# A square block of values with tokens on partitions, kept in DRAM by rows, in a hybrid decoder block on one Trainium2 core

## The chip, the cores and the metric

The kernel runs as one program on one core of a Trainium2 chip. The time is in device microseconds, from the start to the end of an execution on that core. Its engines are TensorE (PE in the profile; its weight loads are PEld), VectorE (DVE), ScalarE (ACT), GpSimd (POOL) and SyncE (SP), which here does little but issue DMAs.

## The reference, cut to what matters

One layer with 1024 tokens, model width 1024, everything in fp32:

```python
h = rms_norm(x, mix_norm_g)                       # (1024 tokens, 1024)
z_a, q, k, v, gate_logits = split(h @ w_in)       # 1536 | 768 | 768 | 768 | 2048 columns
# A: z_a = gelu(z_a); u, v_z = its halves; v_z = rms_norm(v_z) over 768 channels,
#    mixed over chunks of 128 tokens by w_spatial, times u
# B: attention in 3 groups of 4 heads (dilation 1, 4, 16), partial rotary on q and k;
#    the outputs of the groups are mixed by their softmax denominators
merged = sigmoid(g_A) * (y_A @ P_A) + sigmoid(g_B) * (y_B @ P_B)
x = x + merged @ w_out
x = x + (gelu(causal_conv3(h2 @ w_gate)) * (h2 @ w_val)) @ w_down     # h2 = rms_norm(x)
out = rms_norm(x, final_norm_g)
```

The change lies in `h @ w_in` and in what takes over its results.

## The kernel before, in words

**Products.** A fp32 product is made of three passes of fp32r matmuls: each operand is split into a high part (a copy on ACT) and a low part (the difference, on DVE), and high x high, low x high and high x low are added up in PSUM. On top of that the large products use a Strassen scheme with 7 products P1 to P7 in place of 8, on quarters of the operands. For the input projection, x stands transposed (channels on partitions), and its sums of quarters (A11, S2, A12, ...) are made once. The columns of w_in come in pairs of 128: for each pair, in_product (L534) runs P1 to P7, each of 12 matmuls of 128x512 (4 slices of the contraction by 3 passes), with weights as the stationary operand and x as the moving one, so that a result has channels on partitions and 512 tokens in the free dimension. The operand of a product is made ahead: weight sums on DVE (L278 to L288), its high part on ACT (L313), its low part on DVE (L314), in four slots. in_evict (L560) adds the products up on DVE and ACT, and in_final (L645) passes results on.

**The order of pairs.** Values of the gating branch (zv) come first. Two of their three pairs are "lead" pairs: lead_pass (L609, matmuls L618) computes them without Strassen with tokens on partitions while the sums of x are made. The third (FIRST) goes through in_product, and because the spatial mixing needs tokens on partitions, turn_v turns it with 16 PE transposes of 128x128 (L681, copied out by ACT at L682). Then come per attention group g = 1, 2, 0 the pairs qa, qc (queries and keys) and v, whose 256 columns attention() turns likewise with 16 transposes per group (L967, ACT L969); then eight gate pairs (ga) with the three pairs zu after the fourth.

**Work beside the products.** tick() is called after every 6 matmuls (half a product); after(lag, fn) puts a step lag ticks later. So the order of PE's instructions is written out: norm_v (L697: square on ACT, the factor rs_v on POOL, scaling on DVE at L709), spatial (L713: 12 small matmuls pm in two PSUM banks per block of 128 tokens, taken out by DVE at L738), and the steps of Attend (L814: load q and k from DRAM, turn them into parts, scores sc at L863 and L867, softmax, pp = transposed probabilities, pT = their copy out of PSUM at L920 on ACT or L922 on DVE, pu = the product with v at L935). mix_groups (L1033) mixes the outputs of the groups with strided operations on DVE (L1072, L1074); while it runs, wd_step makes the sums of w_down's quarters for its first three slices of the contraction (L1144). The other sums, two per step ff, are made beside the up products of the last stage by wd_beside; each sum is stored to DRAM as wT.

**Queues.** All of PE is in written order. DVE and ACT are in written order from the start to the 18th product (ORDERED); from there a scheduler places their instructions. SP issues nearly all DMAs, in order. PSUM has three banks for accumulators (acc), two for turning and small products (tr, which pm uses too) and, in the first part, three more (ps_d).

Of the kernel before, what the change touches and what calls it, by code (L numbers as in the profile page):

```python
# [11 lines left out]
F32 = mybir.dt.float32  # L12
# [8 lines left out]
P = 128  # L21
# [16 lines left out]
FIRST = 2  # L38
SW = 2 * NH
# [20 lines left out]
def input_pairs():  # L60
# [12 lines left out]
    for p in range(3):  # L73
        pairs.append(("zv", p))
        cols += run(OFF_V + 256 * p, 256)
    for g in GROUPS:
        pairs += [("qa", g), ("qc", g), ("v", g)]
        lead, then = range(0, 8), range(8, 16)
        for dims in (lead, then, range(16, 32)):
            cols += by_dim(OFF_Q, g, dims) + by_dim(OFF_K, g, dims)  # L80
        cols += by_dim(OFF_Q, g, range(32, 64)) + by_dim(OFF_K, g, range(32, 64))
        cols += run(OFF_VV + 256 * g, 256)
    for dt in (0, 1, 2, 3, "zu", 4, 5, 6, 7):
        if dt == "zu":
            for p in range(3):
                pairs.append(("zu", p))
                cols += run(OFF_U + 256 * p, 256)
        else:
            pairs.append(("ga", dt))
            cols += run(OFF_G + P * dt, P) + run(OFF_G + D + P * dt, P)  # L90
    return pairs, cols
# [3 lines left out]
def block_kernel(  # L95
# [15 lines left out]
    w_lead: bass.AP,  # L111
    out: bass.AP,
# [145 lines left out]
    C.append(cxp.tile([P, 2, 1024], F32, name="C2"))  # L258
    OPS_IN = 4
# [66 lines left out]
    ORDERED = 18  # L326
    in_order = [(FIRST, name) for name in ("P1", "P2", "P6", "P7", "P5", "P4")]
    in_order += [(FIRST + 1, "P1"), (FIRST, "P3")]
    in_order += [(FIRST + 1, name) for name in ("P2", "P6", "P7", "P5", "P4", "P3")]
    for n in range(FIRST + 2, NP_IN):  # L330
        in_order += [(n, name) for name in ("P1", "P6", "P2", "P7", "P5", "P4", "P3")]
# [11 lines left out]

    def sums_ahead(i):
        if 7 < i <= ORDERED and in_order[in_ready["op"]] not in summed:
            in_sums(*in_order[in_ready["op"]])
# [159 lines left out]
    def c_tile(n):  # L506
        if n < 5:
            return C[2] if n == FIRST else zv["C"][n - 3]
        return C[(n + 1) % 2]

    def c_half(n, i, h):
        kind, g = PAIRS[n]
        t = c_tile(n)[:, i]
        if kind in ("qa", "qc", "v") and g == 1:
            return t.rearrange("p (r b j) -> p b r j", r=4, b=2)[:, h]
        if kind in ("qa", "qc", "v") and g == 2:
# [3 lines left out]
    def in_turn(n, ap):  # L520

        kind, g = PAIRS[n]
        if kind in ("qa", "qc", "v") and g:
# [3 lines left out]
    FUNC = {"zv": AF.Gelu, "zu": AF.Gelu}  # L527
# [3 lines left out]

    held = []

    def in_product(n, name):  # L534
# [3 lines left out]
        elif name == "P1" or n >= 3:  # L538
            acc = acc_tile(f"in_{n}_{name}")
        else:  # L540
            acc = ps_d.tile([P, HALF], F32, name=f"in_{n}_{name}", tag="dn")
# [11 lines left out]
        if (n, name) == (FIRST, "P4"):  # L553
            held.append(lambda: in_evict(n, name, acc))
        else:
            in_evict(n, name, acc)
            while held:
                held.pop()()
# [86 lines left out]
    def in_final(n, i, h):  # L645
# [3 lines left out]
        if kind == "zv":  # L649
            if (i, h) in ((0, 1), (1, 0)):  # L650
                for bb in range(2):
                    after(5 + bb if h else 4 + bb, lambda b=4 * h + 2 * bb: turn_v(ct, b))
            if (i, h) == (1, 0):
                for b in range(NB):
                    after(7 + 2 * b, lambda b=b: norm_v(b))
                    after(12 + 2 * b, lambda b=b: spatial(b))
        elif kind == "qa":
# [8 lines left out]
        elif kind == "v":  # L666
            if (i, h) == (1, 0):
                attention(p, ct)
# [7 lines left out]
    def turn_v(ct, b):  # L676

        pt = tr_tile(f"vt_{b}")
        for k in range(4):
            o = (b + k // 2) * P  # L680
# [1926 lines left out]
```

## Time and profile before

| | |
|---|---|
| time, median of 3 runs | 1341.72 us (1341.5 to 1342.11) |
| profiled execution | 1342.39 us |
| its span, first to last instruction | 1339.9 us |
| granted TensorE clock | 0.999 of full speed |
| DMA | 241.68 MB, mean 180 GB/s |
| DVE busy, share in the span's 40 slices | 5 to 9 tenths |

In a row of the profile, "L545 PE MATMUL in_P<-R,G 128*128 128x512 f32 x1008 | 237.5, 391 | 0.0" means line 545 of the kernel, engine, operation, output and inputs by tile name without buffer numbers, their shape, the count; then busy us in total, mean ns of one; then the idle time of the engine just before them, with the instruction that ended it. Rows of the waits give what waited, for whom, the total, the number and the longest. The chain is the work that ended last, followed backwards; its rows are start, us, what. Rows of a timeline are start, us, engine, line, operation. Rows of a table of stretches give the stretch, its length and the busy us of PE, PEld, DVE, ACT and POOL (with instruction counts), the granted clock, DMA's share and GB/s.

### The profile page before, as it was taken

What the parts mean: (1) busy time and instruction counts of PE and PEld (TensorE: products, weight loads), DVE (VectorE), ACT (ScalarE), POOL (GpSimd) and SP (SyncE); (2) the same over time, 40 slices, a digit from 0 to 9 for tenths busy, and PEclk for the clock granted to TensorE, in tenths of its full rate; (3) what the DMA queues carried; (4) which work ended last, traced back from release to release, by engine and by line L of the source; (5) the groups of instructions that cost most, each with busy time, mean ns of one, the idle gap of its engine ahead of it and who ended that gap; (6) DMA issues with size and microseconds to landing.
All of it is one profiled execution on the core that took longest, in us unless ns stands there. A gap on an engine that the chain in (4) does not pass through costs nothing.

```text
span 1339.9 us, 18988 instructions
## 1 busy us (share of the span) xinstructions
PE 1327.4 (99%) x6391; PEld 1098.3 (82%) x6391; DVE 1043.4 (78%) x1807; ACT 640.0 (48%) x1242; POOL 281.4 (21%) x271
## 2 busy tenths in 40 slices
PE   9999999999999999999999999999999999999997
PEld 8887887888887888888888788888888888888886
DVE  7988796877779957768889789777777778586674
ACT  7762566666633325345365333433343335454453
POOL 1120000000000000210010336656565653000002
PEclk9999999999999999999999999999999999999999
DMA  9437554555349733975550334454445538996663
GB/s 354 108 103 186 166 152 145 145 155 156 126 134 241 255 127 129 315 232 202 190 166 17 126 101 157 159 165 165 163 151 175 177 116 298 379 336 215 197 204 125
DMA packets 155714, 241.68 MB, mean 180 GB/s; under 512 B 22785, under 2 KB 66274, under 8 KB 155618
## 3 DMA queue, kind: packets, MB, share of 16 engines
q1 hardware_dynamic: 153378, 236.50, 54.8%
q0 software_dynamic: 1088, 2.10, 0.9%
q10 hardware_dynamic: 1152, 1.89, 0.4%
q8 instruction: 50, 0.82, 0.3%
q14 instruction: 46, 0.38, 0.1%
HBM read 172.03 MB, written 64.73 MB: 177 GB/s over the span
## 4 chain that ended last, share of the span: by engine, by line
PE 93%; DVE 3%; ACT 1%; DMA 1%; issue 1%; SPq 1%; POOL 0%; POOLq 0%; DVEq 0%; ACTq 0%
PE in_P L545 26%; PE uP L2020 20%; PE dn L2302 15%; PE up L2020 9%; PE wo_P L1851 5%; PE pa L1481 5%; PE pl L618 3%; PE pu L2000 2%; PE pb L1481 2%; PE pu L935 1%; PE pp L914 1%; PE pm L733 1%; PE sc L863 1%; DMA wr<-in_w_in_dram 1%; PE ht L1755 1%
## 5 line engine op out<-in xcount | busy, mean ns | idle before, releaser
L545 PE MATMUL in_P<-R,G 128*128 128x512 f32 x1008 | 237.5, 391 | 0.0
L545 PEld LDWEIGHTS in_P<-R,G 128*128 128x128 f32 x1008 | 187.3, 188 | 39.3 <-issue 0.5
L2302 PE MATMUL dn<-R 128*128 128x512 f32 x924 | 209.6, 389 | 0.0
L2302 PEld LDWEIGHTS dn<-R 128*128 128x128 f32 x924 | 173.4, 188 | 36.0
L313 ACT ACTIVATE G<-wr 128x512 fp32r<-128x512 f32 x126 | 78.3, 627 | 98.7 <-PE in_P L545 53.5
L170 ACT ACTIVATE R<-up 128x512 fp32r<-128x512 f32 x109 | 65.8, 623 | 123.6 <-DVE up L280 105.5
L2020 PE MATMUL uP<-G,R 128*128 128x512 f32 x504 | 121.3, 389 | 0.8 <-DVE Y L2041 0.8
L545 PE MATMUL in_P<-G,G 128*128 128x512 f32 x504 | 120.8, 392 | 0.6 <-DVE C L580 0.4
L2020 PE MATMUL uP<-R 128*128 128x512 f32 x504 | 121.1, 389 | 0.0
L2020 PE MATMUL up<-G,R 128*128 128x512 f32 x504 | 120.3, 389 | 0.0
L314 DVE TENSOR_TENSOR G<-wr,G 128x512 fp32r<-128x512 f32 x126 | 86.9, 691 | 40.1 <-ACT G L313 38.9
L2020 PEld LDWEIGHTS uP<-G,R 128*128 128x128 f32 x504 | 94.4, 188 | 21.0 <-issue 1.2
L545 PEld LDWEIGHTS in_P<-G,G 128*128 128x128 f32 x504 | 93.4, 188 | 21.7 <-issue 2.0
L2020 PEld LDWEIGHTS uP<-R 128*128 128x128 f32 x504 | 94.6, 188 | 19.7
L2020 PEld LDWEIGHTS up<-G,R 128*128 128x128 f32 x504 | 94.6, 188 | 19.7
L171 POOL TENSOR_TENSOR G<-wbs,G 128x512 fp32r<-128x512 f32 x12 | 17.0, 1431 | 436.0 <-ACT G L170 425.9
L171 POOL TENSOR_TENSOR R<-up,R 128x512 fp32r<-128x512 f32 x55 | 79.4, 1456 | 13.4 <-ACT R L170 12.2
L170 ACT ACTIVATE R<-db 128x512 fp32r<-128x512 f32 x77 | 48.1, 626 | 55.4 <-PE dn L2302 44.5
L171 DVE TENSOR_TENSOR R<-db,R 128x512 fp32r<-128x512 f32 x77 | 53.8, 701 | 25.6 <-ACT R L170 25.6
L1481 PE MATMUL pa<-R,G 128*128 128x512 f32 x288 | 67.9, 389 | 0.0
L545 PE MATMUL in_P<-G 128*128 128x512 f32 x252 | 61.5, 391 | 2.0 <-DVE st L899 1.0
L1481 PEld LDWEIGHTS pa<-R,G 128*128 128x128 f32 x288 | 54.1, 188 | 11.2
(301 smaller groups left out, 2341.8 us busy)
## 6 DMA issues: line engine op xcount, KB each, us to landing
up<-in_w_up_dram SPq DMA_DIRECT2D x44, 512.0 KB, 4.3
wr<-in_w_in_dram SPq DMA_DIRECT2D x42, 512.0 KB, 4.3
dA<-gd SPq DMA_DIRECT2D x55, 256.0 KB, 4.6
dS<-gS SPq DMA_DIRECT2D x44, 256.0 KB, 4.3
db<-wT SPq DMA_DIRECT2D x44, 256.0 KB, 4.5
gd<-Y SPq DMA_DIRECT2D x42, 256.0 KB, 2.0
db<-in_w_down_dram SPq DMA_DIRECT2D x33, 256.0 KB, 4.9
gated<-C SPq DMA_DIRECT2D x32, 256.0 KB, 2.5
```

What stands on the lines that cost most here:

```text
L170: nc.scalar.activation(hi, src, AF.Copy)
L171: fn = lambda: lo_eng.tensor_tensor(lo, src, f32(hi), ALU.subtract)
L313: lambda: nc.scalar.activation(op[:, 0], src, AF.Copy),
L314: lambda: nc.vector.tensor_tensor(op[:, 1], src, f32(op[:, 0]), ALU.subtract),
L545: nc.tensor.matmul(acc, op[:, w, kt, :], left[LEFT[name], kt][:, a, :], start=opened and i == 0, stop=i == len(HIGH_FIRST) - 1, skip_group ...
L618: nc.tensor.matmul(lead_banks[b][:, cs], raw_x[h, kt][:, a, c * P : (c + 1) * P], lead_op(kt, w, cs), start=kt == 0 and p == 0 and cs.star ...
L733: nc.tensor.matmul(acc[hs], v[:, hs], wspT[:, (c * 2 + s) // 3, :], start=True, stop=True)
L1481: nc.tensor.matmul(acc, unit[a][kt // 4][:, kt % 4, :], two(R, 8 * h + kt)[:, b, :], start=n == 0 and i == 0, stop=n == len(kts) - 1 and i ...
L1851: nc.tensor.matmul(acc, left[LEFT[name], kt][:, a, blk * P : (blk + 1) * P], out_ops[s][:, w, :], start=name not in SHARED and kt == 0 and ...
L2000: nc.tensor.matmul(acc, plain_up[which, k][:, w, kt, :], left[f"A{h + 1}{k + 1}", kt][:, a, :], start=n == 0 and i == 0, stop=n == KT - 1 ...
L2020: nc.tensor.matmul(acc, op[w][:, kt, :], left[LEFT[name], kt][:, a, :], start=opened and i == 0, stop=i == len(HIGH_FIRST) - 1, skip_group ...
L2302: nc.tensor.matmul(accs[blk], dops[s][:, 0, a, blk * P : (blk + 1) * P], dops[s][:, 1, w, :], start=SEQ[j] not in CONTINUES and kt == 0 an ...
```

## The change

The last pair of zv and the values of all three groups, 4 pairs or 1024 columns, become one square block, the quad. It is computed at one go as a Strassen product of 1024 tokens by 1024 columns in 28 steps, 7 products (QSEQ) by 4 slices of the contraction: in each step four blocks of 128 tokens by 3 passes, with x as the stationary operand and 512 columns of weights moving. Results have tokens on partitions; quad_result takes them out, stores the values of the groups by rows in a DRAM tensor vd, and starts norm_v on the zv columns, which lie in the same rows. Attention loads its values from vd with plain DMAs (load_v). The transposes of values, and the copies behind them, go. norm_v gets a Gelu of its own per block (before, in_evict's final did that on 128x512).

All else that moves: after the quad the pairs are ordered qa1 qc1 ga0 qa2 qc2 ga1 qa0 qc0 ga2 ga3 ga4 ga5, then zu0 zu1 zu2 ga6 ga7. attention(g) starts as soon as qc of the group is done, with all its steps 4 ticks later (WAIT_QK), where it started after v's seven products. DVE and ACT stay in written order through the quad and four more products. The pT copies are all on ACT. The mix opens after ga5 rather than ga3, a step every 5 ticks, and its adds are contiguous. The 12 sums of w_down beside it go; the up stage makes three per step instead of two, and loads the rows of w_down one at a time.

The core of the diff (new helpers that only load weights or name tiles are left out):

```diff
-    for p in range(3):
+    for p in range(FIRST):
         pairs.append(("zv", p))
         cols += run(OFF_V + 256 * p, 256)
-    for g in GROUPS:
-        pairs += [("qa", g), ("qc", g), ("v", g)]
...
+    pairs += [("quad", k) for k in range(FIRST, QUAD)]
+    cols += run(OFF_VV + 256, 512) + run(OFF_VV, 256) + run(OFF_V + 512, 256)
...
+    rest = [(kind, g) for g in GROUPS for kind in ("qa", "qc", "ga")]
+    rest += ["ga"] * 3 + [("zu", p) for p in range(3)] + ["ga"] * 2
...
-    ORDERED = 18
-    in_order = [(FIRST, name) for name in ("P1", "P2", "P6", "P7", "P5", "P4")]
...
+    ORDERED = 4
+    in_order = []
+    for n in range(QUAD, NP_IN):
         in_order += [(n, name) for name in ("P1", "P6", "P2", "P7", "P5", "P4", "P3")]
...
-        elif kind == "v":
-            if (i, h) == (1, 0):
-                attention(p, ct)
+                attention(p)
...
-    def turn_v(ct, b):
-
-        pt = tr_tile(f"vt_{b}")
-        for k in range(4):
-            o = (b + k // 2) * P
-            nc.tensor.transpose(pt[:, k * P : (k + 1) * P], ct[:, k % 2, o : o + P], ident)
-        nc.scalar.activation(
-            zv["V"][:, b : b + 2], pt.rearrange("p (b c) -> p b c", b=2), AF.Copy
-        )
...
     def norm_v(b):
-        v = zv["V"][:, b]
+        v = last_value(b)
         ms = small.tile([P, 1], F32, name=f"ms_v{b}", tag="ms")
-        nc.scalar.activation(zv["junk"], v, AF.Square, accum_out=ms)
+        nc.scalar.activation(v, v, AF.Gelu)
+        nc.scalar.activation(zv["junk"][:, 0:256], v, AF.Square, accum_out=ms)
...
-        rs = small.tile([P, 1], F32, name=f"rs_v{b}", tag="rs")
-        nc.gpsimd.tensor_tensor(rs, me, mhalf, ALU.pow)
-
-        def scale():
-            for t in (lead_value(b), v):
-                nc.vector.tensor_scalar(t, t, rs, None, ALU.mult)
-
-        after(2, scale)
+        rs_v[b] = small.tile([P, 1], F32, name=f"rs_v{b}", tag="rs")
+        nc.gpsimd.tensor_tensor(rs_v[b], me, mhalf, ALU.pow)
+
+    def scale_v(b):
+        for t in (lead_value(b), last_value(b)):
+            nc.vector.tensor_scalar(t, t, rs_v[b], None, ALU.mult)
...
+    vd = dram.tile([S, 3 * 256], F32, name="vd")
+
+    def v_rows(g, T):
+        cs = vd[:, (g - 1) % 3 * 256 : ((g - 1) % 3 + 1) * 256]
+        if g == 0:
+            return cs[T * P : (T + 1) * P]
+        if g == 1:
+            r, bb = T // 2, T % 2
+            return cs[bb * HALF + r : (bb + 1) * HALF : 4]
+        return cs[T::8]
...
-                if q == 0:
-                    nc.scalar.activation(dst, src, AF.Copy)
-                else:
-                    nc.vector.tensor_copy(dst, src)
+                nc.scalar.activation(dst, src, AF.Copy)
...
         def start(self, s):
+            s += WAIT_QK
             after(max(1, s - 4), self.load)
             after(s, self.turn)
...
+    WAIT_QK = 4
+
+    def attention(g):
         vts = {}
-        def turn_v(T):
-            pt = tr_tile(f"avt_{g}_{T}")
-            for k in range(4):
-                o = (T + k // 2) * P
-                nc.tensor.transpose(pt[:, k * P : (k + 1) * P], ct[:, k % 2, o : o + P], ident)
+        def load_v(T):
             vt = at.tile([P, 2, 256], F32, name=f"v_{g}_{T}", tag="vt", bufs=4)
-            nc.scalar.activation(vt, pt.rearrange("p (t c) -> p t c", t=2), AF.Copy)
-            vts[T], vts[T + 1] = vt[:, 0], vt[:, 1]
-
-        for T, lag in zip(range(0, 8, 2), (5, 7, 10, 12)):
-            after(lag, lambda T=T: turn_v(T), first=True)
+            for t in range(2):
+                nc.sync.dma_start(vt[:, t], v_rows(g, T + t))
+                vts[T + t] = vt[:, t]
+
+        for T, lag in zip(range(0, 8, 2), (8, 12, 16, 20)):
+            after(lag, lambda T=T: load_v(T))
...
-            tt(o, o, wb, ALU.mult)
-            if g:
-                tt(y, y, o, ALU.add)
+            if not g:
+                tt(y, y, wb, ALU.mult)
+                return
+            r = 4 * g
+            wv, ov = wb.rearrange("p (j r) -> p j r", r=r), o.rearrange("p (r j) -> p j r", r=r)
+            tt(wv, wv, ov, ALU.mult)
+            tt(y, y, wb, ALU.add)
...
-            after(6 + 4 * i, lambda step=step: mix(*step))
+            after(6 + 5 * i, lambda step=step: mix(*step))
...
+    QSEQ = ("P1", "P2", "P6", "P5", "P3", "P7", "P4")
...
+    def quad_sum(name, kt):
+        b11, b12, b21, b22 = (quad_raw[i, j, kt] for i in range(2) for j in range(2))
+        tt, sub = nc.vector.tensor_tensor, ALU.subtract
+        if name == "P6":
+            tt(b12, b12, b11, sub)
+            tt(b11, b22, b12, sub)
+        elif name == "P7":
+            tt(b12, b22, b12, sub)
+        else:
+            tt(b21, b21, b11, sub)
+
+    def quad_ahead(n):
+        while quad_done[0] < min(n, 28):
+            s = quad_done[0]
+            op = two(G1, 4 + s % OPS_IN)
+            src = quad_weight(QSEQ[s // QK], s % QK)
+            nc.scalar.activation(op[:, 0], src, AF.Copy)
+            nc.vector.tensor_tensor(op[:, 1], src, f32(op[:, 0]), ALU.subtract)
+            quad_ops[s] = op
+            quad_done[0] += 1
...
+    def quad_result(name, blk, acc):
+
+        u, y = quarter_of(C[2], blk), quarter_of(YC, blk)
+        tt = nc.vector.tensor_tensor
+        rows = [vd[h * HALF + blk * P : h * HALF + (blk + 1) * P] for h in range(2)]
+        if name == "P1":
+            nc.scalar.activation(u, acc, AF.Copy)
+        elif name == "P2":
+            nc.scalar.activation(y, acc, AF.Copy)
+            nc.sync.dma_start(rows[0][:, 0:HALF], y)
+        elif name == "P6":
+            tt(u, u, acc, ALU.add)
+        elif name == "P5":
+            tt(y, u, acc, ALU.add)
+        elif name == "P4":
+            tt(u, u, acc, ALU.add)
+            nc.sync.dma_start(rows[1][:, 0:HALF], u)
+        else:
+            h, t = ((0, zv["Q12"]), (1, zv["Q22"]))[name == "P7"]
+            tt(t[:, blk], u if name == "P3" else y, acc, ALU.add)
+            nc.sync.dma_start(rows[h][:, HALF:], t[:, blk, 0:256])
+            b = 4 * h + blk
+            norm_v(b)
+            after(3, lambda: scale_v(b))
...
+        beside = {
+            0: [lambda: part("S2", 0)], 1: [lambda: part("S2", 1)],
+            2: [lambda: part("S1", 0)],
+            3: [lambda: quad_pair(1, quad_w[1]), lambda: part("S1", 1)],
+            4: [lambda: quad_sum("P6", 0)],
+            5: [lambda: quad_pair(2, quad_w[2]), lambda: quad_sum("P6", 3)],
+            6: [lambda: quad_sum("P6", 1)], 7: [lambda: quad_sum("P6", 2)],
+            8: [lambda: part("S4", 0)], 9: [lambda: part("S4", 1)],
+            10: [lambda: part("S3", 0)], 12: [lambda: part("S3", 1)],
+            13: [lambda: part("A22", 0)], 14: [lambda: part("A22", 1)],
+        }
...
+            op = quad_ops.pop(s)
+            for blk in range(4):
+                for i, (w, a) in enumerate(PASSES):
+                    nc.tensor.matmul(
+                        accs[blk], left[LEFT[name], kt][:, a, blk * P : (blk + 1) * P],
+                        op[:, w, :],
+                        start=name not in SHARED and kt == 0 and i == 0,
+                        stop=kt == QK - 1 and i == 2,
+                        skip_group_check=True,
+                    )
+                if blk % 2:
+                    tick()
+            if kt == QK - 1:
+                for blk in range(4):
+                    quad_result(name, blk, accs[blk])
+            for fn in beside.get(s, ()):
                 fn()
+            quad_ahead(s + 4)
+            if 9 <= s < 13:
+                k = s - 9
+                nc.sync.dma_start(quad_raw[0, 1, k], w_quad[k, :, HALF:])
+            if 13 <= s < 17:
+                quad_sum("P7", s - 13)
+            if 18 <= s < 22:
+                quad_sum("P4", s - 18)
+            if s == 17:
+                square_lead(range(4, 8), zv["junk"])
+            if s >= 14:
+                some(6)
+            if s >= 21:
+                in_ahead(0, 9, max(0, s - 24))
...
+    for b in range(NB):
+        after(1 + 2 * b, lambda b=b: spatial(b))
...
-        if PAIRS[n] == ("v", GROUPS[0]) and name == "P6":
-            while pending:
-                tick()
+        if PAIRS[n] == ("qc", GROUPS[0]) and name == "P3":
...
-        wd_beside(ff - 1 if edge is None else ff, int(edge is not None))
+        wd_beside(ff - 1 if edge is None else ff, 1 + int(edge is not None))
...
+        kt, n = divmod(3 * (ff - WD_FIRST) + place - 1, 4)
+        if not 0 <= kt < NK:
+            return
+        while wd_due:
+            wd_fetch(*wd_due.pop(0))
+        wd_sum(kt, n, [wd_raw.get((kt, q)) for q in range(4)])
```

PE's instructions before, where group 1's attention ends and group 2's begins; avt are the transposes of group 2's values, pp those of probabilities, sc scores, in_9 the products of the pair qa of group 0:

```order
L545 MATMUL in_9_P1_2233<-R_75,G1_76 128x512 x6
L967 MATMUL avt_2_0_2283<-ident_78,C1_104 128x128 x4
L914 MATMUL pp_1_7_0_2291<-ident_78,pr_1_7_2217 128x128 x4
L914 MATMUL pp_1_7_4_2297<-ident_78,pr_1_7_2217 128x128 x4
L545 MATMUL in_9_P1_2233<-R_75,G1_76 128x512 x6
L545 MATMUL in_9_P7_2318<-R_75,G1_76 128x512 x6
L967 MATMUL avt_2_2_2325<-ident_78,C1_104 128x128 x4
L867 MATMUL sc_2_0_2332<-kring_1355,qs_2_0_2268 128x256 x4
L545 MATMUL in_9_P7_2318<-R_75,G1_76 128x512 x6
L545 MATMUL in_9_P5_2360<-G0_77,G1_76 128x512 x12
L967 MATMUL avt_2_4_2378<-ident_78,C1_104 128x128 x4
```

In the changed kernel, PE at the start of group 1's attention, in the two pairs after its qc (in_8 is ga0, in_9 is qa of group 2):

```order
L544 MATMUL in_8_P7_1754<-G0_77,G1_76 128x512 x6
L855 MATMUL sc_1_0_1813<-kring_1676,qs_1_0_1770 128x256 x4
L544 MATMUL in_8_P7_1754<-G0_77,G1_76 128x512 x6
L544 MATMUL in_8_P5_1780<-G1_76 128x512 x12
L544 MATMUL in_9_P1_1879<-R_75,G1_76 128x512 x12
L902 MATMUL pp_1_0_0_1896<-ident_78,pr_1_0_1820 128x128 x4
L851 MATMUL sc_1_1_1902<-kring_1676,qs_1_1_1853 128x256 x8
L544 MATMUL in_9_P6_1927<-R_75,G1_76 128x512 x12
L544 MATMUL in_9_P1_1879<-R_75,G1_76 128x512 x12
L544 MATMUL in_9_P7_1973<-R_75,G1_76 128x512 x6
L902 MATMUL pp_1_1_0_1981<-ident_78,pr_1_1_1913 128x128 x4
L902 MATMUL pp_1_1_4_1987<-ident_78,pr_1_1_1913 128x128 x4
```

The value transposes are gone from between the products, and scores and pp of a group stand beside the products of the next pairs without them.

PE in the changed kernel at the end of the quad; quad_P7 are the four banks that P7 and P4 share, in_6 is the first pair behind the quad, and pm_0_1 and pm_0_0 belong to the spatial mixing of the first block:

```order
L1422 MATMUL quad_P7_0_1022<-G1_76,G0_77 128x512 x3
L1422 MATMUL quad_P7_1_1023<-G1_76,G0_77 128x512 x3
L1422 MATMUL quad_P7_2_1024<-G1_76,G0_77 128x512 x3
L1422 MATMUL quad_P7_3_1025<-G1_76,G0_77 128x512 x3
L544 MATMUL in_6_P1_1222<-R_75,G1_76 128x512 x6
L710 MATMUL pm_0_1_1229<-wspT_895,Q12_878 64x128 x4
L710 MATMUL pm_0_0_1234<-wspT_895,C0_103 64x128 x8
L544 MATMUL in_6_P1_1222<-R_75,G1_76 128x512 x6
L544 MATMUL in_6_P6_1264<-R_75,G1_76 128x512 x6
L710 MATMUL pm_1_1_1271<-wspT_895,Q12_878 64x128 x4
L710 MATMUL pm_1_0_1276<-wspT_895,C0_103 64x128 x8
```

Spatial mixing begins one tick after the quad, where before it began 12 ticks after the last product of the zv pair; each block stands two ticks after the other, as before.

DVE in the changed kernel at that place (L688 scales the values, L323 makes low parts of the operands of in_6, L287 to L289 its weight sums, L1367 takes P4 out):

```order
L688 TENSOR_SCALAR C1_104<-C1_104,rs_v6_1126 128x512
L688 TENSOR_SCALAR Q22_879<-Q22_879,rs_v6_1126 128x256
L688 TENSOR_SCALAR C1_104<-C1_104,rs_v7_1136 128x512
L688 TENSOR_SCALAR Q22_879<-Q22_879,rs_v7_1136 128x256
L323 TENSOR_TENSOR G1_76<-wr_6_0_1064,G1_76 128x512
L287 TENSOR_TENSOR wt3_6_1188<-wr_6_1_1066 128x512
L288 TENSOR_TENSOR wr_6_1_1066<-wr_6_1_1066,wr_6_0_1064 128x512
L289 TENSOR_TENSOR wr_6_0_1064<-wr_6_1_1066 128x512
L323 TENSOR_TENSOR G1_76<-wr_6_0_1064,G1_76 128x512
L1367 TENSOR_TENSOR C2_105<-C2_105,quad_P7_0_1022 128x512
L1367 TENSOR_TENSOR C2_105<-C2_105,quad_P7_1_1023 128x512
L1367 TENSOR_TENSOR C2_105<-C2_105,quad_P7_2_1024 128x512
L1367 TENSOR_TENSOR C2_105<-C2_105,quad_P7_3_1025 128x512
```

The scalings of the last blocks and the operands of in_6 stand before the four evictions of P4, whose last bank pm_0_0 takes over.

342 lines of the change are left out of this document (152 added, 190 removed).

## The prediction

> **What bounds the kernel now.** I read the first part of the page, then the waits of PE, then the chain at the places that the change touches. The page's row of busy times:
>
> ```profile
> PE 1327.4 (99%) x6391; PEld 1098.3 (82%) x6391; DVE 1043.4 (78%) x1807; ACT 640.0 (48%) x1242; POOL 281.4 (21%) x271
> ```
>
> PE works for all but 12 us of the 1339.9 us span; no other engine is near that. So the time is the number of TensorE instructions times their pitch, plus PE's waits. Those that a release explains, from the waits of PE (total us, times, longest):
>
> ```profile
> PE in_P L545 <- DVE st L899: 1.0, 1, 1.0
> PE in_P L545 <- DVE C L582: 1.0, 1, 1.0
> PE in_P L545 <- DVE C L580: 0.4, 1, 0.4
> PE pp L914 <- ACT v L969: 0.3, 1, 0.3
> PE in_P L545 <- DVE G L459: 0.2, 1, 0.2
> ```
>
> They are few: there is little to win by removing waits (2.9 us here), and every microsecond of PE work that goes is worth a microsecond if no new wait eats it. The groups of PE's instructions by line and shape show what goes:
>
> ```profile
> L545 PE MATMUL in_P<-R,G 128*128 128x512 f32 x1008 | 237.5, 391 | 0.0
> L967 PE MATMUL avt<-ident,C 128*128 128x128 f32 x48 | 7.2, 272 | 0.0
> L681 PE MATMUL vt<-ident,C 128*128 128x128 f32 x16 | 2.2, 272 | 0.0
> ```
>
> **What the removed transposes are worth.** The mean of one transpose is 272 ns, but instructions overlap (391 ns for a 128x512 matmul whose share of the busy time is 237.5/1008 = 236 ns). What one holds up is read from the chain (start, us, what) where the third value pair is turned:
>
> ```profile
> 48.42 2.72 PE in_P L545 x12
> ...
> 77.65 0.44 PE vt L681 x4
> 78.09 1.39 PE in_P L545 x6
> 79.48 0.87 PE vt L681 x8
> 80.35 1.39 PE in_P L545 x6
> ```
>
> and where the values of an attention group are:
>
> ```profile
> 210.03 0.68 DVE pT L922
> 210.71 0.60 DVE pr L883
> 211.31 0.03 issue
> 211.34 0.70 DVE qs L849
> ...
> 226.70 0.45 PE avt L967 x4
> 227.15 0.02 issue
> 227.17 0.60 ACT v L969
> ```
>
> Four transposes stand in the chain with 0.44 us, 0.11 us each. The change removes 4 groups of vt and 12 of avt: 16 x 0.44 = **7.0 us**. Matmuls with 512 columns stay at one number (the quad's 28 steps of 12 are 336, as are the four pairs' 4 x 7 x 12), and a dozen of them takes 2.72 us in either order of operands, so nothing else of PE's work changes. The nearest other reading is the busy sum, 7.2 + 2.2 = 9.4 us; I take the chain, since it counts where the next matmul begins. The Trainium skill ("TensorE: Matmul & The Clock Gate", Part 4: PE-mode transpose) gives about 275 ns for one 128x128 transpose in a kernel's context; by that, as time on the path, the 64 would be worth 17.6 us and the kernel would come to about 1326. The trace agrees with that figure as the duration of one (272 ns), but not as what the next instruction waits.
>
> **Waits of before that go.** L459's 0.2 and L580's 0.4 stand in the third value pair's channel products, which no longer exist. The 1.0 before st L899 ends the chain piece at 210 to 213: DVE was behind by a pT copy of 0.68, and all pT copies are now on ACT. The 0.3 of pp is PE behind the copy of the turned values (the 0.60 of v L969). Together **-1.9**. The 1.0 of C L582 lies in the mix stage, whose adds change; I leave it.
>
> **New waits in the quad.** All of DVE's and ACT's work there is written in a fixed order, so I add up pitches by hand: in DVE's timeline dependent sums start 0.72 apart, others 0.60 to 0.61:
>
> ```profile
> 73.11 0.69 DVE L278 TENSOR_TENSOR wt<-wr 128x512 f32<-128x512 f32 x1
> 73.83 0.69 DVE L279 TENSOR_TENSOR wr<-wr,wr 128x512 f32<-128x512 f32 x1
> 74.55 0.69 DVE L280 TENSOR_TENSOR wr<-wr 128x512 f32<-128x512 f32 x1
> 75.16 0.68 DVE L588 TENSOR_TENSOR C<-C,in_P 128x512 f32<-128x512 f32 x1
> ...
> 90.78 0.48 DVE L709 TENSOR_SCALAR C<-C,rs_v 128x512 f32<-128x512 f32 x1
> 91.17 0.35 DVE L709 TENSOR_SCALAR V<-V,rs_v 128x256 f32<-128x256 f32 x1
> 91.43 0.68 DVE L585 TENSOR_TENSOR C<-C,in_P 128x512 f32<-128x512 f32 x1
> ```
>
> Scaling one block of values is 0.39 + 0.26 = 0.65. ACT's square of a 128x256 block and its reading take 0.51 (90.04 to 90.55, where the next instruction starts), and I give the new Gelu of that shape 0.45, an estimate: the row's 0.40 and some gap. So 0.96 a block on ACT:
>
> ```profile
> 90.04 0.40 ACT L700 ACTIVATE junk_v<-V 128x256 bf16<-128x256 f32 x1
> 90.35 0.19 ACT L700 ACTIVATION_READ_ACCUMULATOR junk_v<-V 128x1 f32 x1
> 90.55 1.28 ACT L2518 ACT_TABLE_LOAD   x1
> ```
>
> Operands are made three steps (8.2 us) ahead. After P3 (end of step 19) ACT has four norm chains, 3.8 us, ahead of the high part for step 22: its low part is ready 5.3 us after step 19's end, and needed at 2 x 2.72 = 5.44. No wait. After P7 (end of step 23) DVE has a sum and a low part more in front of the evictions. P4 goes on in P7's banks, so PE waits some 0.45 for the first of them (one low part, 0.6, less what is done by then), and the low part for step 26 is ready 6.3 us after step 23, needed at 5.44 + 0.45: another 0.4. Both: **+0.9** (0 to 2).
>
> Then the end of step 27, E. On DVE, ahead of the evictions of P4, stand the last low parts, eight scalings (4 x 0.65 = 2.6), a low part 0.6, three sums (2.1) and a low part 0.6: 5.9 us that start when the last low part of the quad is done, about E - 3.7. The four evictions start at E + 2.2 and end at E + 4.7. PE after E does six matmuls of in_6_P1 (1.36), four small ones of pm_0_1 (0.25, since 24 of them took 1.53) and comes to pm_0_0 at about E + 1.8. That needs the bank of P4's fourth block. So PE waits **+2.9** there:
>
> ```profile
> 91.78 1.53 PE pm L733 x24
> ```
>
> The ends are 0 (if the scalings find their factors early and everything starts 3 us sooner) and 4.5 (if step 26 is also late on DVE). Behind this wait on PE stand the rest of in_6_P1 and in_6_P6, whose operands are ready; behind the evictions on DVE stand the low parts of the next two operands, needed 5 us later.
>
> **Attention and the DRAM round trips.** Queries and keys go through DRAM as before, but attention(g) now starts at the end of qc, not of v. The page's DMA part (KB each, us to landing):
>
> ```profile
> q<-qd SPq DMA_DIRECT2D x48, 128.0 KB, 3.0
> k<-kd SPq DMA_DIRECT2D x48, 128.0 KB, 2.9
> qd<-C SPq DMA_DIRECT2D x3, 256.0 KB, 3.0
> kd<-C SPq DMA_DIRECT2D x3, 256.0 KB, 4.0
> ```
>
> Eviction 0.7, store 4.0: in DRAM 4.7 us after P3. The loads are issued at tick 4 (4 x 1.36 = 5.4), four of them, about 2 us of SP (an estimate from k's landing share), landed near 10.4; turn stands at tick 8, 10.9. Nothing is late by these medians, with 0.5 us to spare; I set **+1.0** for the three starts (0 to 4). The values by rows are stored in the quad, tens of microseconds before, and loaded from tick 8 for a use at tick 17: hidden.
>
> **w_down sums and the mix.** Twelve sums leave the mix stage for the up stage:
>
> ```profile
> L1144 DVE TENSOR_TENSOR wd<-wd,wd 128x512 f32<-128x512 f32 x12 | 8.3, 688 | 0.9 <-DMA wd<-in_w_down_dram 0.7
> L1144 DVE TENSOR_TENSOR own<-own 128x512 f32<-128x512 f32 x16 | 14.8, 925 | 0.0
> L1144 DVE TENSOR_TENSOR Y<-Y,own 128x512 f32<-128x512 f32 x8 | 8.7, 1085 | 0.0
> ```
>
> A third sum in an up step costs DVE about 1.0 us, not 0.69. One up step in the table of stretches:
>
> ```profile
> 951.24:970.27 19.03, 19.03 (x85) 15.76 (x85) 14.43 (x21) 7.22 (x12) 11.58 (x8) 1.00 0.43 149
> ```
>
> DVE is busy 14.43 of 19.03 us there and PE never waits; 15.4 fit: **0**, unless a row of w_down comes more than 3 us late. The Trainium skill ("GPSIMD Engine Reference", 1. Specifications) says that POOL shares its SBUF interfaces with DVE's instructions of two inputs. The rows agree: 688 ns where POOL has nothing to do, 925 to 1085 beside 11.58 us of POOL. By that rule the move costs DVE 12 x 1.0 instead of 8.3 us, and by neither does it reach PE. In the mix the strided adds become contiguous and the early sums are gone: DVE has less to do; I count 0.
>
> **Sum**, against the profiled execution's 1342.39 us (span 1339.9 and 2.5 around it): -7.0 - 1.9 + 0.9 + 2.9 + 1.0 = -4.1, so 1338.3. The median of the runs is 0.7 lower, 1341.72: **1337.6**. Its own range, from the ends of the waits, is 1335.0 to 1340.2.
>
> **Rivals.**
> - *Full gain.* The factors of the last four blocks are early, pm_0_0 waits under 1 us, the starts cost nothing: -7.0 - 1.9 = -8.9, **1332.8**. For it: DVE has 22% idle; I may have put pitches too high. Against: eight scalings really stand before P4's evictions. 0.20.
> - *The quad is DVE's.* From step 14 on, small operations for the angles come six a step on DVE beside low parts, sums and evictions. If DVE falls 4 to 5 us further behind over the 38 us of these 14 steps (12%), the waits eat all: **1341.7**. For it: L459 and L580 above are just such waits. 0.18.
> - *Slower: the round trip at the three starts.* If store and loads together take longer than the 10.2 us between eviction and turn, ACT stands before the high part of q, and behind it in its queue are the high parts of in-products and the pT copies; PE's scores follow 3 ticks later. Each microsecond over is one of PE, three times. At 4 us over: -8.9 + 3.8 + 12 = +6.9, **1348.6**. It decides from about 1 us over at each start (with 3.8 of quad waits that is still a gain of 2) and from 2.6 over it is slower than before by a measurable amount. For it: 0.5 us is a thin margin, and SP also issues weight loads. Against: medians of 3 to 4 us, and four operands made ahead cover 10.9 us of PE. 0.15.
> - *It doesn't do what it says*: the transposes lay in time that PE would have lost anyway. Against: PE stands at 99% and they are in the chain. 1341.7, 0.03.
> - *Each transpose is worth its duration*, 0.27: **1326** to 1330. 0.02.
>
> **Chances.** Forecast 0.42, and the five as given. A measurement of this kernel tells 0.2% (2.7 us) from no change: faster is below 1339.0, slower above 1344.4. Faster: 0.36 of the forecast's 0.42, with 0.20 and 0.02 and 0.01 of the DVE case, 0.59; slower: 0.15 and 0.02 of the DVE case, 0.17; the rest 0.24. The range leaves out the upper rival, the lowest one and the edges: 1332.3 to 1344.5.
>
> **What would show it.** Right: no transposes of values on PE, PE's busy time lower by 7 us or more, one wait of 2 to 4 us at pm_0_0 for the eviction of P4, a small one in the quad's step 26, and no waits of PE in the up stage. Wrong: several waits of PE on low parts within the quad (the DVE case), on q or k at three places 100 us apart (the round trip), or PE's busy time down by much more or less than 7 us.

## The result, and the profile after

The changed kernel takes 1333.59 us (median of 5 runs, 1333.54 to 1335.28) against 1342.11 for the kernel before on the same chip; the ratio is 0.9941, with a 95% interval of 0.9931 to 0.9952. Its profiled execution is the run of 1333.59 us, with a span of 1331.9 us: 8.0 less than the span of before, where the prediction's sum came to 4.1 less. The time lies in the range that the forecast and its rivals span (1332.3 to 1344.5), but below the forecast's own (1335.0 to 1340.2) and 0.8 above the rival of the full gain (1332.8).

The busy times of the changed kernel, from the first part of its page:

```profile
PE 1319.7 (99%) x6327; PEld 1092.3 (82%) x6327; DVE 1034.3 (78%) x1796; ACT 641.4 (48%) x1243; POOL 282.9 (21%) x271
```

PE has 64 instructions fewer (6391 - 6327) and is busy 7.7 us less. The waits of PE in the changed kernel (total us, times, longest):

```profile
PE pm L710 <- DVE C L1367: 1.8, 1, 1.8
...
PE quad_P L1422 <- DVE Q L1371: 0.8, 1, 0.8
PE uP L2082 <- DVE Y L2103: 0.6, 1, 0.6
PE in_P L544 <- DVE C L576: 0.2, 1, 0.2
PE in_P L544 <- DVE C L574: 0.2, 1, 0.2
```

The two waits at the top are new and stand where the prediction put them: 1.8 at pm_0_0 for P4's evictions, 0.8 at the quad's banks. All of the old ones are gone but that of uP, which the change does not touch: before, they added up to 3.7 with uP, now to 3.6. So the 8.0 us are PE's busy time and hardly the waits. That the new waits come to the same sum as the old ones is an accident: the experiments change one set without the other.

Where the new waits come from is read in DVE's timeline of the changed kernel (start, us, line, operation, idle before):

```profile
114.35 0.48 DVE L688 TENSOR_SCALAR C<-C,rs_v 128x512 f32<-128x512 f32 x1
114.75 0.34 DVE L688 TENSOR_SCALAR Q<-Q,rs_v 128x256 f32<-128x256 f32 x1
115.01 0.69 DVE L1337 TENSOR_TENSOR G<-C,G 128x512 fp32r<-128x512 f32 x1
...
116.81 2.48 DVE L1371 TENSOR_TENSOR Q<-YC,quad_P 128x512 f32<-128x512 f32 x4
121.84 1.29 DVE L1337 TENSOR_TENSOR G<-C,G 128x512 fp32r<-128x512 f32 x2 [2.55 <-ACT G L1336]
123.05 0.48 DVE L688 TENSOR_SCALAR C<-C,rs_v 128x512 f32<-128x512 f32 x1
...
129.43 0.69 DVE L323 TENSOR_TENSOR G<-wr,G 128x512 fp32r<-128x512 f32 x1 [0.76 <-ACT G L322]
130.04 2.48 DVE L1367 TENSOR_TENSOR C<-C,quad_P 128x512 f32<-128x512 f32 x4
```

The quad's last matmul ends at 128.8. P7's evictions (L1371) come behind scalings of the first four blocks and then DVE stands idle for 2.55 us. The scalings of the last four blocks begin at 123.05; P4's evictions (L1367) begin 1.2 us after the quad and end 3.7 after it. The prediction had 2.2 and 4.7.

### The profile page after: what moved, and what is told of

Its sections match the earlier page's. It is cut to its first block, busy times and chain, and to the rows that moved or that the text cites. A ratio compares the mean times of both kernels' runs of the same rounds, so it can differ in the third digit from the quotient of the medians.

```text
span 1331.9 us, 18948 instructions
## 1 busy us (share of the span) xinstructions
PE 1319.7 (99%) x6327; PEld 1092.3 (82%) x6327; DVE 1034.3 (78%) x1796; ACT 641.4 (48%) x1243; POOL 282.9 (21%) x271
## 4 chain that ended last, share of the span: by engine, by line
PE 79%; DVE 1%; ACT 1%; issue 0%; POOLq 0%; DVEq 0%; ACTq 0%; POOL 0%
PE uP L2082 20%; PE in_P L544 17%; PE dn L2374 16%; PE up L2082 9%; PE wo_P L1913 5%; PE pa L1543 5%; PE pu L2062 2%; PE pb L1543 2%; PE pu L920 1%; PE pp L902 1%; PE sc L851 1%; PE ht L1817 1%; PE sc L855 0%; DVE Y L2020 0%; DVE R L179 0%
## 5 line engine op out<-in xcount | busy, mean ns | idle before, releaser
L544 PE MATMUL in_P<-R,G 128*128 128x512 f32 x816 | 192.3, 391 | 0.0
L544 PEld LDWEIGHTS in_P<-R,G 128*128 128x128 f32 x816 | 151.7, 188 | 32.2 <-issue 1.4
L322 ACT ACTIVATE G<-wr 128x512 fp32r<-128x512 f32 x102 | 63.6, 628 | 73.2 <-PE in_P L544 47.8
L544 PE MATMUL in_P<-G,G 128*128 128x512 f32 x408 | 97.9, 392 | 0.2 <-DVE C L574 0.2
L323 DVE TENSOR_TENSOR G<-wr,G 128x512 fp32r<-128x512 f32 x102 | 70.4, 690 | 33.8 <-ACT G L322 32.6
L544 PEld LDWEIGHTS in_P<-G,G 128*128 128x128 f32 x408 | 75.6, 188 | 16.7 <-DVE C L574 0.7
L179 DVE TENSOR_TENSOR R<-up,R 128x512 fp32r<-128x512 f32 x54 | 60.3, 1117 | 1.9 <-ACT R L178 1.9
```

The costliest lines, as they stand in the source:

```text
L179: fn = lambda: lo_eng.tensor_tensor(lo, src, f32(hi), ALU.subtract)
L322: lambda: nc.scalar.activation(op[:, 0], src, AF.Copy),
L323: lambda: nc.vector.tensor_tensor(op[:, 1], src, f32(op[:, 0]), ALU.subtract),
L544: nc.tensor.matmul(acc, op[:, w, kt, :], left[LEFT[name], kt][:, a, :], start=opened and i == 0, stop=i == len(HIGH_FIRST) - 1, skip_group ...
```

## The experiments

"Changed" below is the changed kernel, "before" the kernel before; each time is a median, and each kernel was timed in turns with the kernel before, whose medians were 1341.5 to 1342.8.

**Do the removed transposes explain the gain?** First, as many transposes put in again, where they can't make another engine work:

```diff
-                for i, (h, s) in enumerate(self.blocks[q : q + 4]):
+                again = 2 if doubled[0] < 16 else 1
+                doubled[0] += 1
+                for i, (h, s) in list(enumerate(self.blocks[q : q + 4])) * again:
                     nc.tensor.transpose(
```

> The changed kernel with the transposes of probabilities of the first 16 groups of four done twice into the same bank: 64 transposes more, as many as the change removed, and nothing for another engine. Theory (0.11 us each on PE's path): 1333.6 + 7.0 = 1340.6. Rivals: each costs its duration of 272 ns, +17.4, 1351.0; or they lie in time that PE loses anyway, 1333.6.

Measured 1341.32, ratio to before 1.0 (0.9991 to 1.0008): +7.7 against the changed kernel. The duration (+17.4) and the free transposes (0) are out. In the chain of before, a group of four and one of eight transposes of probabilities:

```profile
198.93 0.59 PE pp L914 x4
...
207.29 0.87 PE pp L914 x8
```

and in the chain of this kernel, groups of the same two sizes, doubled:

```profile
226.14 1.02 PE pp L906 x8
...
234.95 1.75 PE pp L906 x16
```

Four more take 0.43 us, eight more 0.88: 0.11 each, 7.0 for 64. By the first part of the page PE is busy 6.4 us longer (1326.1 against 1319.7), and one wait on an eviction is 1.3 us where it was 0.2, so even work that falls on PE alone shifts its neighbours.

Then the other way round, the transposes alone, with the copies behind them, taken from before:

```diff
-            pt = tr_tile(f"avt_{g}_{T}")
-            for k in range(4):
...
-            nc.scalar.activation(vt, pt.rearrange("p (t c) -> p t c", t=2), AF.Copy)
+            nc.sync.dma_start(vt, w_lead[T // 2].rearrange("p (t c) -> p t c", t=2))
```

and the same in the turn_v of the zv pair.

> The kernel before without its 64 transposes of values and their 16 copies on ACT; the tiles are filled by plain DMAs from a weight input instead, so the values are left out and all else stays, the order of pairs, the mix and the w_down sums too. Theory (most of the gain is the transposes): 16 x 0.44 = 7.0 and the wait of 0.3 on the turned values go, 1342.1 - 7.3 = 1334.8. Rival (most of the gain came with the new order and the mix): less than 3 us of gain, over 1339.

Measured 1337.0 against 1341.5, ratio 0.9961 (0.9948 to 0.9975): -4.5, neither theory's 7.3 nor the rival's under 3. The five runs go from 1334.75 to 1338.23, so the size is known to some 2 us only; the interval, 3.4 to 7.0 us, leaves out both. Its waits say where the rest went:

```profile
PE in_P L545 <- DVE st L895: 2.1, 2, 1.3
...
PE in_P L545 <- DVE C L582: 1.1, 2, 1.0
PE in_P L545 <- DVE C L580: 1.0, 2, 0.6
PE pm L729 <- POOL me_v L699: 0.8, 1, 0.8
```

Waits of 5.0 us stand where before had 2.4 (1.0 st, 1.0 C L582, 0.4 C L580). The one at pm is made by the substitute: its square on ACT waits 3.27 us for the DMA that stands in for the transposes. The others are for DVE's work, on which PE, coming earlier, waits longer: 1.1 more on st, in two stretches of attention, and 0.7 more on evictions ahead of the mix. That DVE is what is short at st is shown by e9 below. PE's busy time is 6.5 us less than before (1320.9).

**What the other parts of the change are worth.** Two small ones alone in the kernel before:

```diff
-                if q == 0:
-                    nc.scalar.activation(dst, src, AF.Copy)
-                else:
-                    nc.vector.tensor_copy(dst, src)
+                nc.scalar.activation(dst, src, AF.Copy)
```

> The kernel before with all copies of turned probabilities on ACT, as in the changed kernel. Theory (a copy of 0.68 us on DVE is what makes PE wait 1.2 us at 212 us): that wait falls to 0.3 to 0.5, 1342.1 - 0.8 = 1341.3. Rival (other DVE work of that stretch makes it): no change, 1342.1.

Measured 1340.33 against 1341.51, ratio 0.9991 (0.9982 to 1.0): -1.2, at the edge of what shows. In its waits the one on st is gone:

```profile
PE in_P L545 <- DVE C L582: 1.0, 1, 1.0
PE wo_P L1848 <- ACT Y L1816: 0.9, 1, 0.9
PE uP L2017 <- DVE Y L2038: 0.3, 1, 0.3
PE pp L914 <- ACT v L966: 0.3, 1, 0.3
```

The one of 0.9 at wo_P lies in a stage that the edit does not touch and is in no other run's list here.

```diff
-            tt(o, o, wb, ALU.mult)
-            if g:
-                tt(y, y, o, ALU.add)
+            if not g:
+                tt(y, y, wb, ALU.mult)
+                return
+            r = 4 * g
+            wv, ov = wb.rearrange("p (j r) -> p j r", r=r), o.rearrange("p (r j) -> p j r", r=r)
+            tt(wv, wv, ov, ALU.mult)
+            tt(y, y, wb, ALU.add)
```

> The kernel before with the mix's adds contiguous, as in the changed kernel; its spacing of four ticks and the twelve early w_down sums stay. Theory (the waits of 0.5 and 1.1 us at 426 and 430 us come from strided adds on DVE, 1.14 us against 0.69): both fall, 1342.1 - 1.4 = 1340.7. Rival (they come from late loads before, or from the place of the mix beside zu): no change, 1342.1.

Measured 1339.62 against 1341.51, ratio 0.9986 (0.9978 to 0.9995): -1.9, the two waits and a little more. The waits that are left have neither C L580 nor C L582:

```profile
PE in_P L545 <- DVE st L899: 0.8, 1, 0.8
PE uP L2020 <- DVE Y L2041: 0.3, 1, 0.3
PE pp L914 <- ACT v L969: 0.3, 1, 0.3
PE in_P L545 <- DVE G L459: 0.2, 1, 0.2
```

So the strided adds on DVE made PE wait in the mix. The chain of before has a product (L1072) and its add (L1074) at the place, between the evictions L580 and L582:

```profile
426.26 0.60 DVE C L580
...
427.46 1.12 DVE ob L1072
...
429.19 1.05 DVE YC L1074
430.24 0.58 DVE C L582
...
430.95 5.27 PE in_P L545 x22
```

PE's two waits there are those of 0.4 on C L580, up to 427.00, and of 1.0 on C L582, up to 430.95. In the kernel before, a product and its add took (groups by line and shape; the second number is the mean in ns)

```profile
L1074 DVE TENSOR_TENSOR YC<-YC,ob 128x512 f32<-128x512 f32 x8 | 9.1, 1135 | 0.1
L1072 DVE TENSOR_TENSOR ob<-ob,wb 128x512 f32<-128x512 f32 x8 | 9.1, 1132 | 0.1
```

and in the changed kernel

```profile
L1058 DVE TENSOR_TENSOR wb<-wb,ob 128x512 f32<-128x512 f32 x8 | 8.7, 1087 | 1.3 <-DMA ob<-od 1.3
L1059 DVE TENSOR_TENSOR YC<-YC,wb 128x512 f32<-128x512 f32 x8 | 5.5, 689 | 0.1
```

8 x 0.45 = 3.6 us of DVE less. The Trainium skill ("SBUF — State Buffer", Door 1: The DMA port swizzle, in a note there) says that consecutive accesses run at full bandwidth within a line of 16 bytes and that each new line pays a penalty. The rows agree: the strided views of the adds in the kernel before step 4 or 8 fp32 values, 16 bytes or more, and take 1135 ns where contiguous ones take 689. The product L1058 keeps a strided operand in the changed kernel, and still takes 1087.

All three in the kernel before:

> The kernel before with the three edits at once: no transposes of values (the values are left out, tiles filled by DMAs from a weight input), copies of probabilities on ACT, contiguous adds in the mix. Theory: the terms add up, -7.3 - 0.8 - 1.4 = -9.5, 1332.6, which is lower than the changed kernel, since the quad's two new waits (2.6) aren't there and the value stage's old ones (0.6) are. Rival (the quad or the new order of pairs carries a gain of its own): clearly above that, 1334.8 or more.

Measured 1332.99 against 1341.51, ratio 0.9939 (0.9927 to 0.9951): -8.5. PE's busy time is that of the changed kernel (1319.7), 7.7 us less than before. With DVE relieved at the two places, the waits on st (2.1 in e5) and those in the mix (1.3) are gone. One by one the three edits gave 4.5, 1.2 and 1.9, together 7.6; that they give more at once than that can't be told from times with this spread. The waits:

```profile
PE pm L729 <- POOL me_v L699: 0.8, 1, 0.8
PE uP L2009 <- DVE Y L2030: 0.7, 1, 0.7
PE in_P L545 <- DVE C L580: 0.4, 1, 0.4
PE in_P L545 <- DVE C L582: 0.2, 1, 0.2
```

The old order of pairs with these three edits is as fast as the changed kernel (1333.59), though it leaves the values out. So the quad as it stands, with its two new waits, carries no further gain; it is the way to have values without turning them. Both sides have waits of their own making (0.8 at pm here, 2.6 there), and without its two the quad is ahead (e3, next).

**Are the two new waits worth their size?** Three edits of the changed kernel, e1, e2 and both:

```diff
-        after(1 + 2 * b, lambda b=b: spatial(b))
+        after(3 + 2 * b, lambda b=b: spatial(b))
```

> The changed kernel, with the spatial mixing two ticks (2.7 us) later: PE comes to pm_0_0 about 4.1 us after the quad's last step instead of 1.4, and the evictions of P4 end 3.7 us after it. Theory (PE waits there only because it comes too early): the wait of 1.8 us goes and nothing takes its place, so 1333.6 - 1.8 = 1331.8. Rival (the wait is DVE's backlog, which only shows at the first place that meets it): PE waits as long at the next product's operand or bank, 1333.6.

```diff
-            after(3, lambda: scale_v(b))
+            if h:
+                after(3, lambda: scale_v(b))
+            if b == 7:
+                for bb in range(4):
+                    scale_v(bb)
```

> The changed kernel, with the scalings of the first four blocks written behind P7's evictions instead of ahead of them. In the profile after, eight scalings (2.6 us) stand on DVE ahead of these evictions, and DVE is idle for 2.55 us behind them. Theory: the wait of 0.8 us on quad_P for Q goes, 1333.6 - 0.8 = 1332.8, and the wait at pm stays at 1.8. Rival (low parts, not scalings, hold DVE up): no change, 1333.6; or the wait at pm grows by what the other loses.

> The changed kernel with both edits, the spatial mixing two ticks later and the first four scalings behind P7's evictions. Theory: the two waits are separate, both go, 1333.6 - 2.6 = 1331.0. Rival (one backlog of DVE): the gain of the better one alone, 1331.8, or none, 1333.6.

| kernel | us | ratio to before | PE waits in its profile |
|---|---|---|---|
| changed | 1333.59 | 0.9941 (0.9931 to 0.9952) | pm 1.8, quad_P 0.8 |
| e1 | 1331.11 | 0.9925 (0.9912 to 0.9937) | quad_P 0.7 |
| e2 | 1332.16 | 0.9929 (0.9917 to 0.9942) | pm 1.5 |
| e3 | 1330.10 | 0.9917 (0.9903 to 0.9931) | neither |

-2.5, -1.4 and -3.5: both waits go, and nothing takes their place. That they go is read in the profiles; what each is worth is less sure, as the intervals of e1 and e2 overlap that of the changed kernel, and by the ratios the three gains are 2.1, 1.6 and 3.2. Within that they add up. All of e3's waits, but that on the identity at the start, are

```profile
PE uP L2086 <- DVE Y L2107: 0.6, 1, 0.6
PE in_P L544 <- DVE C L576: 0.3, 1, 0.3
```

e3 is the fastest kernel here, by 0.83% of the one before.

**The round trip at the starts of attention**, the prediction's slower rival:

```diff
-    WAIT_QK = 4
+    WAIT_QK = 0
```

> The changed kernel with the four extra ticks at the start of attention taken away (WAIT_QK 0): the first scores of a group stand 7 ticks (9.5 us) after qc's last product instead of 11 (15.0 us). Theory of the prediction (the round trip of q and k through DRAM sets that margin): store landed some 4.5 us after the product, loads of 2 us issue and 3 us landing, 2 us to make parts, so scores are ready at about 11.5 to 12 and PE waits some 2 us at each of the three starts: 1333.6 + 6 = 1339.6. Rival (the margin is ample, the trip is hidden in any case): no change, 1333.6.

Measured 1336.66, ratio 0.9968 (0.9955 to 0.9980): +3.1 against the changed kernel. The mechanism is there, at half the size:

```profile
PE sc L855 <- DVE kring L179: 2.9, 2, 2.0
```

Two of the three starts wait, 2.0 and 0.9 us. So four ticks (5.4 us) leave 3.4 us even at the worst start. The prediction counted the margin up to turn only, 0.5 us; what is left of the three ticks from turn to the scores belongs to it as well.

**Do strided adds still cost in the new order?**

```diff
-            r = 4 * g
-            wv, ov = wb.rearrange("p (j r) -> p j r", r=r), o.rearrange("p (r j) -> p j r", r=r)
-            tt(wv, wv, ov, ALU.mult)
-            tt(y, y, wb, ALU.add)
+            tt(o, o, wb, ALU.mult)
+            if g:
+                tt(y, y, o, ALU.add)
```

> The changed kernel with the strided adds of the mix put back; its spacing of five ticks stays, and the early w_down sums stay away. Theory (strided adds are what made PE wait in the mix of before, where flat adds alone gave 1.9 us): waits of 0.5 to 1.5 us come back beside zu, 1333.6 + 1.0 = 1334.6. Rival (five ticks and the missing sums leave DVE enough room): no change, 1333.6.

Measured 1336.79, but the five runs go from 1334.2 to 1337.96: not settled. The three above 1336 have a mean granted clock of 0.997, the two below 1335 one of 0.999; the profiled one, the longest, shows what that is, at the end of this document. The two below 1335 lie 0.6 and 1.3 above the changed kernel. On e3 it was asked again:

> The strided adds of the mix once more, now on the version with both edits (spatial mixing later, first scalings later), which has no wait at pm and so, if the drop of the granted clock to 0.5 between 133 and 137 us in the previous two profiles comes from that wait, no such drop either. Theory (with five ticks and no early sums the strided adds cost only the 0.4 us wait that the earlier profile shows beside zu): 1330.1 + 0.4 = 1330.5, and a spread of the runs of about 1 us. Rival (the strided adds cost as much as in the kernel before): 1330.1 + 1.9 = 1332.0. Rival on the clock (its drops have nothing to do with the wait): single runs 2 to 4 us above the others, as before.

Measured 1331.6 (1330.7 to 1333.35), ratio 0.9919 (0.9905 to 0.9932), which e3's interval covers: 1.5 by the medians, 0.3 by the ratios. In the profile the evictions' wait is

```profile
PE in_P L544 <- DVE C L576: 1.3, 2, 0.8
```

1.0 more than in e3. One of the two, 0.8, stands at 459 us in the mix, behind a strided add; e3 has none there. The other, 0.5 at 245 us, lies ahead of the mix, where e3 has its 0.3. So the adds cost about 0.8 us here as well, between theory and rival; five ticks and the missing sums are not the whole of it.

**The copies of probabilities in the changed kernel**, the second of a block on DVE again:

```diff
-                nc.scalar.activation(dst, src, AF.Copy)
+                if q == 0:
+                    nc.scalar.activation(dst, src, AF.Copy)
+                else:
+                    nc.vector.tensor_copy(dst, src)
```

> The changed kernel with the second copy of turned probabilities of a block on DVE again. Theory (the copy stands on DVE ahead of the evictions that PE waits for): the two waits of 0.2 on the evictions C grow to about 1 each, 1333.6 + 1.2 = 1334.8, the size that moving it gave in the kernel before. Rival (with the turned values' copies gone and other neighbours, its place does no harm): no change, 1333.6.

Measured 1334.37 (1334.02 to 1337.15), +0.8. The profile has one wait of 0.9 on C L576 where the changed kernel had 0.2 and 0.2: the mechanism shows, its size can't be told from the spread.

## Why the prediction was right, step by step

The direction, the cause and the places of the new waits were right; the size was not: the gain by the medians is 8.5 us, twice the 4.1 of the sum. Nearly all terms erred the same way, each by about 1 us or less, so the measured time came near the rival of the full gain, whose condition (under 1 us at pm_0_0) isn't met. That the time lies in the outer range owes more to the rivals than to the forecast.

- **PE's path is the time**: right. PE is 99% busy in both profiles, and in each of the 14 profiles here the span is PE's busy time and its waits, the one at the start with them, and 6.9 to 7.3 us more.
- **Transposes, -7.0**: right. By doubling they cost 0.11 us each (e4); taken away, they lower PE's busy time by 6.5 us (e5). That DVE's waits can eat the gain was in the rivals, for the quad only; e5 shows it elsewhere: 1.8 us on DVE, and 0.8 that the substitute makes. (The aside on the duration comes to 1327.0 by the sum's other terms, not to 1326.)
- **Waits that go, -1.9**: too small. I left the 1.0 of C L582 in the mix standing because I counted 0 for the lighter DVE there. And I misplaced the 0.4 of L580: it stands at 427 us in the mix, not in the third value pair, and went for the same reason as C L582, not for mine. So the mix held 1.4 us of waits, and flat adds alone are worth 1.9 (e8).
- **Quad, +0.9 before the end**: 0.8 in the profile, all of it at P7's banks; the second half, step 26 late, didn't happen. The scalings of the first four blocks made it (e2), not the sum and the low part that I named. So that the size came out is luck.
- **pm_0_0, +2.9**: the place, the cause and the order of DVE's work were right; 1.8 in the profile. The scalings began at 123.05, not at 125.1 (3.7 before the quad's end), since the last low parts were done early, and DVE's idle time of 0.76 before the last low part was not in my sum. PE came to pm_0_0 1.9 us after the quad, near the 1.8 that I gave, though my terms add up to 1.6: pm_0_1 is 8 records of 64 ns (1.53 / 24), 0.5 us, where I counted 4.
- **Attention, +1.0**: nothing for q or k. The two waits of 0.2 are for evictions, 0.4 in all, a cause that I had not named.
- **w_down sums, 0**: right. A step of the up stage in the changed kernel, in the table of stretches:

```profile
951.00:970.00 19.00, 19.00 (x86) 15.73 (x85) 15.02 (x22) 7.22 (x12) 11.57 (x8) 1.00 0.57 186
```

DVE is busy 15.02 us where it was 14.43, with one instruction more, and PE still never waits.

- **The range, 1335.0 to 1340.2**: it is said to come from the ends of the waits, but it is 2.6 to either side. The ends that I gave (0 to 2, 0 to 4.5, 0 to 4) add up to 1332.8 to 1343.3, and the measured 1333.59 lies in that.

Added up against -4.1: 1.1 from pm, 0.6 from attention, 0.1 from the quad, 1.2 from waits that went (C L582's 1.0, and 0.2 less at uP): -7.1. The span moved by 8.0. Most of what is left is PE's busy time, which fell by 7.7 where the transposes make 7.0. Where these 0.7 us lie stays open: with 64 transposes put in, e4's rose by only 6.4.

## What to carry to other kernels

On a kernel whose PE is 99% busy, removing PE work is worth its pitch in the chain (the time until the next instruction starts), not the duration of a row, and only where the engine that feeds PE has room: look at that engine's queue at the next place where PE will be early. When a new order is written out, add up the pitches of what stands ahead of each eviction; a wait at a first small product can be had back by moving that product a few ticks later, as in e1. And an access with a stride on a side engine can stand behind a wait of the main one.

## What was not expected of the hardware

In the profiles of e11 and e12 the granted clock falls to half just behind the wait at pm. e11, by stretches:

```profile
129.00:133.00 4.00, 2.40 (x17) 1.57 (x15) 3.24 (x6) 1.68 (x3) 0.00 (x0) 1.00 0.21 78
133.00:135.00 2.00, 1.80 (x18) 1.49 (x19) 2.00 (x6) 0.00 (x0) 0.00 (x0) 0.78 1.00 371
135.00:137.00 2.00, 2.00 (x7) 1.54 (x5) 1.97 (x6) 0.00 (x0) 0.00 (x0) 0.50 0.35 93
137.00:140.00 3.00, 3.00 (x31) 2.42 (x29) 1.05 (x3) 1.91 (x6) 0.00 (x0) 0.91 0.28 75
```

and the changed kernel, with the same wait of 1.8 us and its clock at 1.00:

```profile
129.00:133.00 4.00, 2.18 (x22) 1.47 (x22) 3.57 (x6) 1.44 (x3) 0.00 (x0) 1.00 0.38 138
133.00:135.00 2.00, 2.00 (x20) 1.61 (x15) 2.00 (x8) 0.00 (x0) 0.00 (x0) 1.00 0.68 253
135.00:137.00 2.00, 2.00 (x16) 1.45 (x16) 1.56 (x4) 1.71 (x6) 0.00 (x0) 1.00 0.66 180
```

In e12 the drop begins at 132.6, as PE goes on after the wait, and lasts to 136:

```profile
129.00:132.00 3.00, 1.77 (x14) 1.06 (x12) 2.54 (x5) 1.46 (x3) 0.00 (x0) 1.00 0.15 53
132.00:134.00 2.00, 1.41 (x14) 1.41 (x16) 2.00 (x5) 0.00 (x0) 0.00 (x0) 0.65 1.04 386
134.00:136.00 2.00, 2.00 (x10) 1.38 (x7) 1.64 (x7) 0.00 (x0) 0.00 (x0) 0.50 0.43 132
```

The drop lasts some 3.4 us in both. In e12 the time from the start of the pm that had waited to the next block's is 5.58 us, in the changed kernel 3.97, so it costs 1.6 us on top of the wait. What PE does just before doesn't decide it: from 129 to 132 us PE is busy 1.77 us in e12 and 1.75 in the changed kernel, with a pause up to 132.59 and 132.57 in them, and only one of the two drops. Of the profiles with a wait of about 1.5 us or more at pm it shows in two and not in four (changed, e2, e4, e6); of the three others in the new order (e1, e3, e13) in none. The Trainium skill ("TensorE: Matmul & The Clock Gate", Part 1: The HAM clock gate) says that activity is looked at in free-running windows of about 3.4 us. By that the same wait can fall into one window or be shared by two, which would fit a drop in some executions only. That the wait is its cause is not settled: one run of e13, which has no such wait, is 1.3 us above the others, for a reason that no profile here shows.
